# The MLP of a float32 decoder trunk: chunks of W1 interleaved with K tile pairs of W2, both column halves by seven products, sums moved in and out of PSUM

## The chip, the cores and the metric

The kernel runs on one core of one Trainium2 chip, as one program. The metric is the device time of an execution in microseconds. Before the change the runs took 2034.95, 2032.8 and 2032.91 us; their median is 2032.91 us. Each profile is of one further execution.

## What is computed

Two layers over 256 positions of width 2048, in float32. Layer 0 mixes by a gated short convolution, layer 1 by multi-head latent attention. Each mixer and each MLP is followed by a layer norm of `ALPHA * h + f(h)`. The part that the change touches is the MLP of both layers:

```python
def sq_relu_mlp(x, w1, w2):
    return jnp.square(jax.nn.relu(x @ w1)) @ w2    # x: 256 x 2048, w1: 2048 x 8192, w2: 8192 x 2048
```

## The kernel before, in words

**Numbers.** A float32 value is held as a pair: `hi` (rounded to fp32r by ScalarE) and `lo` (the rest, by a VectorE subtraction); `split` (L120) makes one pair and is two instructions. Each product is then three matmuls, hi·hi, hi·lo and lo·hi. Where the moving operand is the activations, its hi and lo lie side by side, so hi·(hi, lo) is one matmul of 512 columns (`high`, L199) and lo·hi is one of 256 columns (`low`, L203). Where the moving operand is the weights, the three are matmuls of 512 columns (`dot`, L271).

**The stream of weights.** All weights come through one list, `stream` (L75), in the order of their use. A *unit* is a tile of 128 x 1024 floats (512 KB), loaded by SyncE into one of five `raw` buffers and split into one of eight pairs of `hi`/`lo` buffers. `take` (L182) hands out the next items and, ahead of them, calls `prepare` (L146) for later items up to five tiles ahead (`LOOK`).

**The MLP before** (`mlp`, L550) goes by eight quarters `q` of 1024 hidden columns. In each, eight *chunks* of 128 hidden columns are made (`products`, L253, called with `lag=False`, so that `high` and `low` alternate for each of the 16 K tiles); a chunk is evacuated by `whole` (L327: a ScalarE copy of one half of the bank, a VectorE add of the other) and then by Relu, Square and a split. In quarter 0 the chunks are made from the not yet normalised input (`mm_wide`). Then the quarter's four *pairs* of K tiles are multiplied by W2. W2's 2048 columns are four blocks of 512 (n = 0 to 3).

- A plain pair-half (two K tiles, two token halves, two column blocks) is 8 `dot`s. `down` (L286) does it block by block, in two PSUM banks.
- A fast pair-half is done by 7 products in place of 8 (a Winograd form of Strassen's scheme on 2 x 2 blocks). `down_fast` (L314) does it, in seven PSUM banks, with the order in `FACTORS` (L311). It needs three more forms of W2 (T1 to T4 with B11, B22 and B21; L161 to L176), and four more of the hidden values (S1 to S4, L604 to L607). For each fast pair-half `prepare` has VectorE do one subtraction of 1024 elements (L165), two of 512 (L168, L171), three `lo` of 1024 and one of 512, and ScalarE the `hi` of the same.
- Before, only columns 0 to 1023 go the fast way, and only in the quarters `FAST` (L36): quarters 1 to 6 of layer 0, 1 to 7 of layer 1. Each has 4 pairs, so that is 24 and 28 fast pair-halves of the 64 in a layer.

At the end of each quarter `combine` (L639) and `put` (L567) add the PSUM sums to `acc` in SBUF, on VectorE. `to_wide` (L655) and `to_out` (L900) take the last quarter of layers 0 and 1; in layer 1 `turn_residual` (L892) puts the transposed residual into `acc` ahead of the last quarter.

**Order.** The tile framework allocates buffers, sets every wait, and orders each engine's queue. Its order can differ from that of the source: in the trace L605 of one pair runs before L331 that the source puts ahead of it.

Of the kernel before, what the change touches and what calls it, by code (L numbers as in the profile page):

```python
# [31 lines left out]
LOOK = 5  # L32
# [3 lines left out]
FAST = {0: range(1, NQ - 1), 1: range(1, NQ)}  # L36
FIRST = ((0, 2, 4, 8), (0, 4, 8))
GROUP = 3
# [4 lines left out]
LAG = 16  # L43
# [4 lines left out]
def trunk(ctx: ExitStack, tc: tile.TileContext, xT, vecs, w_in, w_out, w_kv, w_q, w_uk, w_uv,  # L48
# [12 lines left out]
    ROOM = {"a1": 16896, "a2": 16896, "b": 33280, "c": 16384}  # L61
# [8 lines left out]
    def halves(w):  # L70

        lead = len(w.shape) - 2
        return [(w,)] if lead == 0 else [h for i in range(w.shape[0]) for h in halves(w[i])]
# [5 lines left out]

    def mlp_stream(l):  # L80
        out = []
        for q in range(NQ):
            out += halves(w1[l, q * QC:(q + 1) * QC])
            lead = 0
            if q in FAST[l]:
                out += [(w2f[l, q, j, 0], w2f[l, q, j, 1]) for j in range(QC // 2)]
                lead = 2
            out += halves(w2[l, q, lead:])
        return out
# [4 lines left out]
    stream += halves(w_o) + mlp_stream(1)  # L94

    class Banks:


        more, count = None, 0
# [12 lines left out]
        @classmethod  # L112
        def next(cls):
            cls.count += 1
            return cls.more if cls.more is not None and cls.count % 8 >= 4 else pmm

    state = {"split": 0, "next": 0}
# [13 lines left out]
    def load(i, raw, cuts):  # L131

        hi, lo = ready[i] = parts(i)
        for b0, b1 in zip(cuts, cuts[1:]):
            at, cols = slice(b0, b1), slice(P * b0, P * b1)
            nc.sync.dma_start(raw[:, cols], stream[i][0][:, cols])
            yield
            split(hi[:, at, :], lo[:, at, :], tiled(raw[:, cols]))
            yield
# [6 lines left out]
    def prepare(i):  # L146

        if len(stream[i]) == 1:
            raw = load_raw(i, stream[i][0])
            hi, lo = ready[i] = parts(i)  # L150
            split(hi, lo, tiled(raw))
            return
        r1, r2 = (load_raw(f"{i}_{j}", src) for j, src in enumerate(stream[i]))
        out = []

        def finished(r, name):
            hi, lo = parts(name)
            split(hi, lo, tiled(r))
            out.append((hi, lo))

        b22, (b21, b12) = r1[:, BW:], (r2[:, :BW], r2[:, BW:])  # L161
        finished(r1, f"{i}_1")
# [4 lines left out]
        finished(t, f"{i}_t")  # L167
        nc.vector.tensor_tensor(b12, b22, t[:, :BW], ALU.subtract)  # L168
        finished(r2, f"{i}_2")
        t4 = r1[:, :BW]  # L170
        nc.vector.tensor_tensor(t4, b21, b12, ALU.subtract)  # L171
        f = state["fast"].tile([P, 2, BW], F32R, tag="t4", name=f"t4_{i}")
        split(f[:, 0, :], f[:, 1, :], t4)
        b1, t13, b2 = ([[v.rearrange("p b c -> p (b c)")[:, o:o + BW] for v in w] for o in (0, BW)] for w in out)
        ready[i] = {"11": b1[0], "22": b1[1], "21": b2[0], "T2": b2[1], "T1": t13[0], "T3": t13[1],
                    "T4": [f[:, 0, :], f[:, 1, :]]}  # L176

    def size(i):

        return 1 if len(stream[i]) == 1 else 3  # L180

    def take(halves=2):  # L182

        i = state["next"]
        state["next"] += halves
        ahead = -sum(size(j) for j in range(i, i + halves))
        for j in range(i, len(stream)):
            ahead += size(j)
            if ahead > LOOK:
                break  # L190
            if j >= state["split"]:
                prepare(j)
                state["split"] = j + 1
        return [ready.pop(i + j) for j in range(halves)]
# [12 lines left out]
    def mm_run(wps, x, k0, k1, nk, tiles_first=False, turn=None):  # L207
# [4 lines left out]
        for k, (w, ps) in order:  # L212
            if k == turn:
                low(ps, w, k, x[k], False)
                high(ps, w, k, x[k], False)
                continue
            high(ps, w, k, x[k], k == 0)
            low(ps, w, k, x[k], k == nk - 1)

    def mm_lag(ps, w, x):  # L220

        for k in range(NC + LAG):
            if k < NC:
                high(ps, w, k, x[k], k == 0)
            if k >= LAG:
                low(ps, w, k - LAG, x[k - LAG], k == NC + LAG - 1)

# [25 lines left out]
    def products(n, x, group=0, cuts=(), turn=None, lag=True):  # L253
# [7 lines left out]
        for i in range(group, n):  # L261
            w = take()
            ps = psum("ps_u")
            if lag:
                mm_lag(ps, w, x)
            else:
                mm_run([(w, ps)], x, 0, NC, NC, turn=turn if i == 0 else None)
# [3 lines left out]
    def dot(ps, w, x, first, last):  # L271

        nc.tensor.matmul(ps, x[0], w[0], start=first, stop=False)  # L273
        nc.tensor.matmul(ps, x[0], w[1], start=False, stop=False)  # L274
        nc.tensor.matmul(ps, x[1], w[0], start=False, stop=last)  # L275
# [34 lines left out]

    FACTORS = (("4", "22", "T4"), ("2", "12", "21"), ("3", "S4", "22"), ("1", "11", "11"),  # L311
               ("6", "S2", "T2"), ("7", "S3", "T3"), ("5", "S1", "T1"))

    def down_fast(x, forms):  # L314

        ps = {p: psum(f"ps_f{p}") for p, _, _ in FACTORS}
        n = len(x) // 2
        for j in range(n):
            b, = take(1)
            a = {"11": held(x[2 * j], 0), "12": held(x[2 * j + 1], 0), "22": held(x[2 * j + 1], 1)}  # L320
            for i in range(4):
                a[f"S{i + 1}"] = [v[:, j, (4 + i) * P:(5 + i) * P] for v in forms]
            for p, l, r in FACTORS:
                dot(ps[p], b[r], a[l], j == 0, j == n - 1)
        return ps
# [191 lines left out]
    state["split"] = 2 * GROUP  # L517
# [32 lines left out]
    def mlp(idx, ln, begin, blocks, fast):  # L550
# [12 lines left out]

        def block(n, t):
            return acc[:, t, n * BW:(n + 1) * BW]

        def put(n, t, ps):  # L567
            if q == 0:
                nc.scalar.copy(block(n, t), ps)
                for _ in range(2):  # L570
                    normal()
            else:
                nc.vector.tensor_tensor(block(n, t), block(n, t), ps, ALU.add)

        for q in range(NQ):
            forms = [array(a, F32R, f"h{idx}_{q}_{a}", QC // 2, 8 * P) for a in ("c", "a2")] if q else None
            if q == NQ - 1:
                begin(block)
            if forms is None:
                ht = array("c", F32R, f"h{idx}_{q}", QC, 2 * T)  # L580
                h = [ht[:, k, :] for k in range(QC)]
            else:
                h = [tuple(v[:, k // 2, (k % 2) * T:(k % 2 + 1) * T] for v in forms) for k in range(QC)]

            def hidden(m, ps, evac, *func):
                if forms is None:
                    f = tmp.tile([P, T], F32, tag="fh", name="fh", bufs=3)
                else:
                    if m % 2 == 0:
                        state["pair"] = fast.tile([P, 8 * P], F32, tag="sf", name="sf")  # L590
                    f = state["pair"][:, m % 2 * T:(m % 2 + 1) * T]
                evac(ps, f, *func)
                if not func:
                    nc.scalar.activation(f, f, AF.Relu)  # L594
                nc.scalar.activation(f, f, AF.Square)
                if forms is None:
                    put_split(h[m], f)
                elif m % 2:
                    hi, lo = (v[:, m // 2, :] for v in forms)
                    src, cols = state["pair"], 4 * P  # L600
                    if q in FAST[idx // 2]:
                        cols = 8 * P
                        a11, a21, a12, a22, s1, s2, s3, s4 = (src[:, i * P:(i + 1) * P] for i in range(8))
                        nc.vector.tensor_tensor(s1, a21, a22, ALU.add)  # L604
                        nc.vector.tensor_tensor(s3, a21, a11, ALU.subtract)  # L605
                        nc.vector.tensor_tensor(s2, s1, a11, ALU.subtract)
                        nc.vector.tensor_tensor(s4, a12, s2, ALU.subtract)  # L607
                    split(hi[:, :cols], lo[:, :cols], src[:, :cols])

            if q == 0:  # L610
                for m in range(QC):
                    if m < GROUP:
                        if m == 0:
                            ws = ln.ws if ln.ws else group_of(GROUP)
                            if not ln.ws:
                                mm_wide(ws, ln.xd)
                            ln.finish()
# [6 lines left out]
                    if m > 0:  # L624
                        normal()
# [393 lines left out]
```

## Time and profile before

| | us |
|---|---|
| median of three runs | 2032.91 |
| the profiled execution | 2034.58 |
| its span, first to last instruction | 2032.5 |
| PE busy, 11208 matmuls | 2013.5 |
| VectorE (DVE) busy | 1654.6 |
| ScalarE (ACT) busy | 1181.9 |
| moved by DMA | 385.31 MB |

The profile lists engines as PE (matmul), PEld (weight load, beside PE), DVE, ACT, POOL and SP. A group's row gives line, engine, operation, output<-inputs, shape and count; then the busy time in us, the mean ns of one, and the idle time just before. Consecutive instructions of one engine overlap by some tens of ns, so costs per instruction are read from start to start. A matmul's listed length is longer still than its pace, since matmuls are pipelined.

### The profile page before, as it was taken

To read this page: it belongs to the slowest core of one execution; us is meant where nothing else is said; L and a number is where in the kernel's file an instruction comes from. 1 tells how busy PE (TensorE), PEld (TensorE's weight loads), DVE (VectorE), ACT (ScalarE), POOL (GpSimd) and SP (SyncE) were. 2 spreads that over 40 slices of the span, in tenths; PEclk is the share of its full clock that TensorE was granted. 3 is DMA by queue.
4 is the path that set the end of the run, shared out by engine and by line. 5 is a ranking of instruction groups with operands and counts; after the bars stand their busy time and mean duration, and the time that the engine had idled before them with its cause. 6 is when DMAs were issued, how large, how long until landed. Compare 5 with 4: busy or idle time off the path is not lost.

```text
span 2032.5 us, 30055 instructions
## 1 busy us (share of the span) xinstructions
PE 2013.5 (99%) x11208; PEld 1760.0 (87%) x11208; DVE 1654.6 (81%) x2494; ACT 1181.9 (58%) x1752; POOL 2.3 (0%) x21
## 2 busy tenths in 40 slices
PE   9999999999999999999999999999999999999997
PEld 7888888988888888888889998898888888888885
DVE  7667667677898988989688888777889898898988
ACT  6444445576565565655556655467656566565652
POOL 0000000000000000000000000000000000000000
PEclk9999999999999999999999999999999999999998
DMA  8666656564746557475754534656475665746644
GB/s 297 204 190 189 191 189 190 166 202 139 254 145 227 181 182 254 145 233 174 230 176 149 176 122 134 199 171 201 137 248 152 221 210 161 250 145 224 206 164 152
DMA packets 108002, 385.31 MB, mean 190 GB/s; under 512 B 11984, under 2 KB 13392, under 8 KB 107856
## 3 DMA queue, kind: packets, MB, share of 16 engines
q1 hardware_dynamic: 107712, 383.13, 58.8%
q8 instruction: 88, 1.44, 0.3%
q14 instruction: 58, 0.48, 0.1%
q10 hardware_dynamic: 144, 0.26, 0.0%
HBM read 381.25 MB, written 2.10 MB: 189 GB/s over the span
## 4 chain that ended last, share of the span: by engine, by line
PE 96%; DVE 2%; DMA 1%; issue 1%; ACT 0%; DVEq 0%; ACTq 0%
PE ps_u L201 32%; PE ps_u L205 17%; PE ps_d L273 7%; PE ps_d L274 7%; PE ps_d L275 7%; PE ps_f L274 4%; PE ps_f L275 4%; PE ps_f L273 4%; PE ps_w L247 1%; PE ps_w L245 1%; PE ps_w L246 1%; PE ps_g L247 1%; PE ps_g L245 1%; PE ps_g L246 1%; DMA raw<-in_w2f_dram 1%
## 5 line engine op out<-in xcount | busy, mean ns | idle before, releaser
L123 DVE TENSOR_TENSOR lo<-raw,hi 128x1024 fp32r<-128x1024 f32 x712 | 856.9, 1221 | 257.7 <-ACT hi L122 179.9
L122 ACT CAST hi<-raw 128x1024 fp32r<-128x1024 f32 x712 | 743.6, 1051 | 486.4 <-PE ps_u L201 268.9
L201 PE MATMUL ps_u<-xhl,hi 128*128 128x512 f32 x1792 | 622.1, 392 | 0.0
L205 PE MATMUL ps_u<-xhl,lo 128*128 128x256 f32 x1792 | 499.6, 280 | 0.0
L201 PEld LDWEIGHTS ps_u<-xhl,hi 128*128 128x128 f32 x1792 | 334.4, 187 | 73.1
L205 PEld LDWEIGHTS ps_u<-xhl,lo 128*128 128x128 f32 x1792 | 338.6, 189 | 1.7
L273 PE MATMUL ps_d<-hi,h_c 128*128 128x512 f32 x480 | 186.8, 389 | 0.0
L275 PE MATMUL ps_d<-hi,h_a 128*128 128x512 f32 x480 | 186.6, 389 | 0.0
L274 PE MATMUL ps_d<-lo,h_c 128*128 128x512 f32 x480 | 186.6, 389 | 0.0
L201 PE MATMUL ps_u<-xhl_a,hi 128*128 128x512 f32 x720 | 171.9, 391 | 0.0
L201 PEld LDWEIGHTS ps_u<-xhl_a,hi 128*128 128x128 f32 x720 | 132.4, 188 | 25.7
L274 PEld LDWEIGHTS ps_d<-lo,h_c 128*128 128x128 f32 x480 | 90.1, 188 | 18.8 <-DVE lo L123 0.2
L275 PEld LDWEIGHTS ps_d<-hi,h_a 128*128 128x128 f32 x480 | 90.1, 188 | 18.7
L273 PEld LDWEIGHTS ps_d<-hi,h_c 128*128 128x128 f32 x480 | 90.1, 188 | 18.6
L205 PEld LDWEIGHTS ps_u<-xhl_a,lo 128*128 128x128 f32 x720 | 92.3, 191 | 3.5
L594 ACT ACTIVATE sf<-sf 128x256 f32<-128x256 f32 x112 | 46.7, 417 | 82.1 <-DVE sf L331 81.9
L205 PE MATMUL ps_u<-xhl_a,lo 128*128 128x256 f32 x720 | 93.4, 283 | 0.0
L122 ACT CAST hi_t<-raw_t 128x1024 fp32r<-128x1024 f32 x52 | 54.6, 1050 | 47.1 <-DVE raw_t L165 32.0
L330 ACT COPY t<-ps_u 128x256 f32<-128x256 f32 x157 | 57.0, 363 | 42.1 <-PE ps_u L205 42.1
L274 PE MATMUL ps_f<-lo,h_c 128*128 128x512 f32 x208 | 81.2, 390 | 0.2 <-DVE lo L123 0.2
L275 PE MATMUL ps_f<-hi,h_a 128*128 128x512 f32 x208 | 81.1, 390 | 0.0
L273 PE MATMUL ps_f<-hi,h_c 128*128 128x512 f32 x208 | 80.7, 389 | 0.0
(235 smaller groups left out, 3290.8 us busy)
## 6 DMA issues: line engine op xcount, KB each, us to landing
raw<-in_w_dram SPq DMA_DIRECT2D x408, 512.0 KB, 4.4
raw<-in_w2f_dram SPq DMA_DIRECT2D x104, 512.0 KB, 3.6
raw<-in_w_in_dram SPq DMA_DIRECT2D x90, 512.0 KB, 4.2
raw<-in_w_out_dram SPq DMA_DIRECT2D x32, 512.0 KB, 4.0
raw<-in_w_o_dram SPq DMA_DIRECT2D x32, 512.0 KB, 4.1
raw<-in_w_kv_dram SPq DMA_DIRECT2D x10, 512.0 KB, 4.2
raw<-in_w_q_dram SPq DMA_DIRECT2D x8, 512.0 KB, 4.4
raw<-in_w_uk_dram SPq DMA_DIRECT2D x8, 512.0 KB, 4.5
```

The lines of the kernel that those rows point to most:

```text
L122: nc.scalar.copy(hi, src)
L123: nc.vector.tensor_tensor(lo, src, hi.bitcast(F32), ALU.subtract)
L201: nc.tensor.matmul(ps, w[blk // 8][0][:, blk % 8, :], x, start=first, stop=False)
L205: nc.tensor.matmul(ps[:, :T], w[blk // 8][1][:, blk % 8, :], x[:, :T], start=False, stop=last)
L245: nc.tensor.matmul(ps[:, :W], hi, x[k][:, :W], start=k == 0, stop=False)
L246: nc.tensor.matmul(ps[:, :W], lo, x[k][:, :W], start=False, stop=False)
L247: nc.tensor.matmul(ps[:, :W], hi, x[k][:, W:], start=False, stop=k == NC - 1)
L273: nc.tensor.matmul(ps, x[0], w[0], start=first, stop=False)
L274: nc.tensor.matmul(ps, x[0], w[1], start=False, stop=False)
L275: nc.tensor.matmul(ps, x[1], w[0], start=False, stop=last)
L330: nc.scalar.copy(t, ps[:, T:])
L594: nc.scalar.activation(f, f, AF.Relu)
```

## The change

The quarters go. After the first eight chunks a plan alternates one *group* (one pair-half of W2) with one chunk of W1, to the end of the 28 first pairs (`KEPT`); the three chunks that remain follow, and the last four pairs are done by `down` in all four column blocks.

- **Fast almost everywhere.** Both column halves (b = 0: columns 0 to 1023; b = 1: the others) go the fast way, save the pairs in `PLAIN`: 0 and 1 in both halves, and 4, 8, 12, 16, 20, 24 in half 1. A layer has 46 fast and 10 plain groups.
- **Turns.** The halves take turns of four pairs (the first turn is of two). The seven sums of one half stay in seven PSUM banks; at a turn ScalarE copies each to a slot of 512 columns in SBUF (`spill`) and copies the other half's back into the bank (`seed`), and the next matmuls go on adding to it. A plain group inside half 1 uses bank 1 for C22, so one spill and one seed stand after it too.
- **Folding once a layer.** `fold` and `combine` add the seven sums up at the end, in 16 VectorE adds; before, each quarter did so.
- **One bank for W1.** While the seven banks are held, all chunks of W1 share the eighth (`Banks.only`).
- **Chunks** are now 8 `high`, 8 `low`, 8 `high`, 8 `low` (`mm_like`). In the mixers 16 `high` and then 16 `low` follow each other, as before.
- **The stream** is prepared tile by tile (`prepare` is a generator) up to eight tiles from the start of the item in use. `sf` and `t4` have two buffers, each other buffer count is kept.
- **Moved:** the norm's preparation of layer 0 is spread over the groups, the other half of the normalised input is made in the first four groups, and `turn_residual` now comes after the fold.

```diff
+PAIRS = FF // (2 * P)
+KEPT = PAIRS - QC // 2
+SLOTS = 10
+PLAIN = ((0, 1), (0, 1, *range(4, KEPT, 4)))
...
+    def plan():
+        nxt, b, steps, m, count = [0, 0], 0, [], QC, 0
+        while min(nxt) < KEPT:
+            end = min(nxt[b] + (4 if nxt != [0, 0] else 2), KEPT)
+            run = [(b, j, j in PLAIN[b]) for j in range(nxt[b], end)]
+            for i, (b, j, plain) in enumerate(run):
+                steps.append(("group", b, j, plain, i == 0, i == len(run) - 1))
+                if count >= 3 and m < FF // P:
+                    steps.append(("m", m))
+                    m += 1
+                count += 1
+            nxt[b], b = end, 1 - b
+        return steps + [("m", i) for i in range(m, FF // P)]
...
+        while state["made"] < min(start[i] + WA, start[-1]):
+            next(making)
+            state["made"] += 1
...
+    def mm_like(ps, w, x, n=NC):
+        for h in range(0, NC, n):
+            for k in range(h, h + n):
                 high(ps, w, k, x[k], k == 0)
+            for k in range(h, h + n):
+                low(ps, w, k, x[k], k == NC - 1)
...
+    FAST = (("1", "11", "11"), ("3", "S4", "22"), ("7", "S3", "T3"), ("5", "S1", "T1"),
+            ("2", "12", "21"), ("6", "S2", "T2"), ("4", "22", "T4"))
...
+        def spill(self, p):
+            if p in self.live:
+                nc.scalar.copy(self.slot(self.live.pop(p)), self.bank[p])
+
+        def seed(self, p, key):
+            if key in self.store:
+                nc.scalar.copy(self.bank[p], self.at(key))
+                self.drop(key)
+                self.live[p] = key
...
+        def turn(self, b, plain):
+            for p, _, _ in FAST:
+                if p in self.bank:
+                    self.spill(p)
+                    self.seed(p, (b, "C" if p == "1" and plain else p))
...
+            if step[0] == "m":
+                w, ps = take(), psum("ps_m")
+                mm_like(ps, w, xhl, 8)
...
+                whole(ps, half)
+                if m % 2:
+                    nc.scalar.activation(f[:, :4 * P], f[:, :4 * P], AF.Relu)
+                    square(f)
...
+            w, = take(1)
+            later = [s for s in steps[at + 1:] if s[0] == "group"]
+            turns = plain and bool(later) and not later[0][3]
+            sums.group(b, w, parts_of(j), plain, last, turns)
+            if later:
+                if last:
+                    sums.turn(later[0][1], later[0][3])
+                elif turns:
+                    sums.spill("1")
+                    sums.seed("1", (b, "1"))
```

More of the change, by code (lines that the diff above doesn't have):

```diff
@@ L31 @@
 NEG = -1e30
-LOOK = 5
 RAW, WA = 5, 8
@@ L94, in trunk @@
     stream += halves(w_o) + mlp_stream(1)
+    size = {"unit": 1, "plain": 2, "fast": 3}
+    start = [0]
+    for kind, *_ in stream:
+        start.append(start[-1] + size[kind])
     class Banks:
-        more, count = None, 0
+        more, count, only = None, 0, None
         @classmethod
@@ new lines, in mlp @@
+        sums = Sums(idx)
+        Banks.only = Banks.more
+        count = 0
+        for at, step in enumerate(steps):
+            if step[0] == "m":
+                m = step[1]
+                w, ps = take(), psum("ps_m")
+                mm_like(ps, w, xhl, 8)
+                if m % 2 == 0:
+                    f = pair()
+                half = f[:, m % 2 * T:(m % 2 + 1) * T]
+                whole(ps, half)
+                if m % 2:
+                    nc.scalar.activation(f[:, :4 * P], f[:, :4 * P], AF.Relu)
+                    square(f)
+                    j, cols = m // 2, 4 * P
+                    if j < KEPT:
+                        forms(f)
+                        cols = 8 * P
+                    split(one[:, j % 4, :cols], two[:, j % 4, :cols], f[:, :cols])
+                if m == FF // P - 3:
+                    Banks.only = None
+                continue
+            _, b, j, plain, first, last = step
+            w, = take(1)
[8 more added lines that the diff above has]
+                    sums.seed("1", (b, "1"))
+            if first and j + 4 >= KEPT and b == 0 and j + 2 >= KEPT:
+                folded = sums.fold(1)
+            if not later:
+                folded = sums.combine(0) + folded
+            if count < 4:
+                normal()
+                normal()
+            if hook is not None:
+                hook(count)
+            count += 1
@@ L564, in block @@
         def block(n, t):
-            return acc[:, t, n * BW:(n + 1) * BW]
+            return folded[n][t]
         def put(n, t, ps):
[L568 to L617, printed above, removed]
-                        ps = ws[m][1]
-                    else:
-                        ws = [(take(), psum("ps_w"))]
-                        mm_wide(ws, ln.xd)
-                        ps = ws[0][1]
-                    hidden(m, ps, ln.weighted, AF.Relu)
-                    if m > 0:
-                        normal()
-                acc = array("a1", F32, f"acc{idx}", 2, D)
-            else:
-                for m, ps in enumerate(products(QC, xhl, turn=2, lag=False)):
-                    hidden(m, ps, whole)
-            if q == NQ - 1:
-                blocks(block, put, h, forms)
-                return
-            if q in FAST[idx // 2]:
-                combine(put, down_fast(h, forms))
-            for n in range(2 if q in FAST[idx // 2] else 0, NB):
-                down(h, put, n)
@@ L657, in turned, with to_wide @@
+        h = [(one[:, k // 2, k % 2 * T:(k % 2 + 1) * T], two[:, k // 2, k % 2 * T:(k % 2 + 1) * T]) for k in range(QC)]
+        blocks(block, put, h)
+    def to_wide(block, put, h):
         def turned(n):
```

273 lines of the change are left out of this document (169 added, 104 removed).

## The prediction

> **What bounds the kernel now.** I read the page's totals and slices first, then who waits for whom, then the pace of PE in each kind of stage, then what the other engines have left there.
>
> ```profile
> span 2032.5 us, 30055 instructions
> ...
> PE 2013.5 (99%) x11208; PEld 1760.0 (87%) x11208; DVE 1654.6 (81%) x2494; ACT 1181.9 (58%) x1752; POOL 2.3 (0%) x21
> ...
> DVE  7667667677898988989688888777889898898988
> ```
>
> PE has no hole, and the DVE digits show 8 and 9 just in the two MLPs: a second engine is close behind. PE's waits are few:
>
> ```profile
> PE ps_g L201 <- DVE xhl_a L336: 2.5, 2, 1.7
> PE warm L349 <- DVE col L351: 1.1, 1, 1.1
> PE ps_g L201 <- ACT hi L122: 0.8, 1, 0.8
> PE lnAB L372 <- DVE rr L367: 0.3, 1, 0.3
> ```
> ```profile
> PE 96%; DVE 2%; DMA 1%; issue 1%; ACT 0%; DVEq 0%; ACTq 0%
> ```
>
> (Waits: total us, times, longest; those left out are shorter. Below them the chain that ended last, by engine.) Time goes down one for one with matmuls removed, as long as the others feed PE.
>
> A "busy" PE counts modelled lengths, so its pace is read from starts. Two timelines of PE, `dot`s and an MLP chunk (first and last row of 57 and of 27 starts), and the chain in the mixer:
>
> ```profile
> 519.68 0.39 PE L274 MATMUL ps_f<-lo,h_c 128*128 128x512 f32 x1
> ...
> 532.37 0.39 PE L273 MATMUL ps_d<-hi,h_c 128*128 128x512 f32 x1
> ```
> ```profile
> 477.79 0.39 PE L201 MATMUL ps_u<-xhl,hi 128*128 128x512 f32 x1
> ...
> 486.80 0.39 PE L201 MATMUL ps_u<-xhl,hi 128*128 128x512 f32 x1
> ```
> ```profile
> 99.77 3.65 PE ps_u L201 x16
> 103.42 1.91 PE ps_u L205 x16
> ```
>
> A `dot` matmul: 12.69 us / 56 = 0.2266 us. An alternating `high`/`low` pair: 9.01 / 26 = 0.3465, so 5.545 us a chunk. Sixteen of each in a row: 3.65 + 1.91 = 5.56 us. So a fast group is 21 x 0.2266 = 4.76 us, a plain one 24 x 0.2266 = 5.44 us.
>
> How near DVE is shows in stretches of one fast quarter each (length, PE, PEld, DVE, ACT busy):
>
> ```profile
> 544.40:629.80 85.40, 85.40 (x439) 73.03 (x438) 74.41 (x96) 51.81 (x70) 0.00 (x0) 1.00 0.61 199
> 629.80:715.20 85.40, 85.40 (x439) 73.08 (x438) 73.86 (x96) 50.89 (x70) 0.00 (x0) 1.00 0.60 195
> ```
>
> DVE 87%, ACT 60%, PE without a wait, clock 1.00.
>
> **The change, part by part.** *Removed matmuls.* Fast pair-halves go from 24 + 28 = 52 to 46 + 46 = 92. Forty `dot`s fewer, 120 matmuls, 11088 in all: 120 x 0.2266 = **-27.2 us**.
>
> *Chunk order.* 112 chunks from 5.545 to 5.56: **+1.7** (0 to 3; with 8 and 8 it lies between the two rows).
>
> *DVE.* Costs from start to start come from the groups (busy, mean ns) and from unbroken runs, one of DVE and one of ACT:
>
> ```profile
> L123 DVE TENSOR_TENSOR lo<-raw,hi 128x1024 fp32r<-128x1024 f32 x712 | 856.9, 1221 | 257.7 <-ACT hi L122 179.9 <-issue 38.4 <-PE ps_u L205 37.5
> ...
> L165 DVE TENSOR_TENSOR raw_t<-raw,raw 128x1024 f32<-128x1024 f32 x52 | 63.4, 1220 | 4.5 <-DMA raw<-in_w2f_dram 4.2
> L573 DVE TENSOR_TENSOR acc<-acc,ps_f 128x512 f32<-128x512 f32 x78 | 52.1, 681 | 0.4
> L331 DVE TENSOR_TENSOR sf<-ps_u,t 128x256 f32<-128x256 f32 x112 | 46.8, 418 | 0.3 <-ACT t L330 0.3
> L573 DVE TENSOR_TENSOR acc<-acc,ps_d 128x512 f32<-128x512 f32 x60 | 40.4, 684 | 3.8 <-PE ps_d L275 3.7
> L171 DVE TENSOR_TENSOR raw<-raw 128x512 f32<-128x512 f32 x52 | 35.6, 686 | 0.5
> ...
> L573 DVE TENSOR_TENSOR acc<-acc,vu 128x512 f32<-128x512 f32 x39 | 25.6, 684 | 0.0
> ...
> L606 DVE TENSOR_TENSOR sf<-sf 128x128 f32<-128x128 f32 x52 | 15.0, 288 | 0.9
> ```
> ```profile
> 517.21 3.49 DVE L123 TENSOR_TENSOR lo<-raw,hi 128x1024 fp32r<-128x1024 f32 x3
> ```
> ```profile
> 513.71 1.05 ACT L122 CAST hi<-raw 128x1024 fp32r<-128x1024 f32 x1
> 514.66 0.62 ACT L122 CAST t<-raw 128x512 fp32r<-128x512 f32 x1
> 515.18 1.99 ACT L122 CAST hi<-raw 128x1024 fp32r<-128x1024 f32 x2
> ```
>
> Three `lo` take 3.49, where three lengths are 3.66, so each overlaps the next by 0.085: DVE pays 1.135 us for 1024 elements, 0.60 for 512, 0.335 for 256, 0.20 for 128. ACT pays 0.95 for 1024, 0.52 for 512.
>
> - Fast group, DVE: three `lo` and one subtraction of 1024, one `lo` and two subtractions of 512: 4 x 1.135 + 3 x 0.60 = 6.34 us. Plain group: 2.27.
> - Chunk: two `lo` and the add of `whole`, 2.6; for every second chunk the S forms (0.2 + 0.335 + 0.2) and a split of 1024, so 0.93 a chunk.
> - A step of group and chunk: fast 9.88 us of DVE beside 4.76 + 5.56 = 10.32 of PE; plain 5.81 beside 11.0.
>
> A cycle of eight steps, a turn of each half, has seven fast and one plain: **DVE 75.0, PE 83.2 us, 90%**. So DVE alone doesn't become the bound, though it has less left than now. It is given back the adds of each quarter (78 + 60 + 39 of L573 at about 0.60, against 24 per layer); the fold's 16 lie beside the last groups and chunks.
>
> *ACT and the turns.* A turn is 7 spills and 7 seeds. By the plan a layer has 12 full turns, two part ones and the pairs of copies after plain groups: 195 copies, 390 in all. The nearest row for a spill is the second one here, a copy out of PSUM of that shape; the first is the copy of `whole`:
>
> ```profile
> L330 ACT COPY t<-ps_u 128x256 f32<-128x256 f32 x157 | 57.0, 363 | 42.1 <-PE ps_u L205 42.1
> ...
> L569 ACT COPY acc<-ps_d 128x512 f32<-128x512 f32 x16 | 9.0, 582 | 4.2 <-PE ps_d L275 3.9
> ```
>
> 582 ns less the same overlap is 0.49. A copy into PSUM is in no row; between that row and the cast (0.52) I take 0.52, so a turn is 7 x 1.01 = 7.1 us. By the Trainium skill, "ScalarE: Activation LUTs", section "What ACT_TABLE_LOAD costs", an ACTIVATE with immediate operands takes 186 ns + 0.833 ns per element and overlaps the next by 93 ns; that would make 0.52 us of each copy (an estimate) and 7.3 us of a turn, and this trace's 582 ns lies just under it.
>
> ACT per cycle: fast step 3 x 0.95 + 0.52, chunk 1.9 + 0.3 (363 ns less the overlap), half of (Relu, Square, split of 1024) 1.0, so 6.6; plain 5.1; with two turns and one extra pair 7 x 6.6 + 5.1 + 15.2 = 66.5 of 83.2, 80%.
>
> The copies wait for PE: a spill of a bank waits for that bank's last `dot`, 0.68 us after the one before, while a spill and a seed take 1.01, so ACT is held 7.1 us and ends some 8 us after the group began. PE comes back to bank 1 after 10.3 us: the seeds themselves hide behind the chunk. What is queued behind them on ACT are the casts of the next tiles; DVE's `lo` waits for these:
>
> ```profile
> DVE lo L123 <- ACT hi L122: 183.6, 179, 5.6
> ...
> ACT hi L122 <- DMA raw<-in_w_dram: 126.0, 137, 2.8
> ```
>
> Call s the time that DVE idles in a turn: at most 7.1. Meanwhile it can do the next fast pair's first two subtractions (1.74), a chunk's add (0.33) and one or two `lo` whose cast is ready (1.1 to 2.3): 3.2 to 4.3 us, so s is 2.8 to 3.9. The cycle then needs 75.0 + 2s = 80.6 to 82.8 us of DVE, just inside PE's 83.2. Eight buffers of tiles cover the turn itself. Timing isn't that even (loads land late, an odd chunk costs 1.9 more than an even one), so I take 0.3 us of PE wait for each of 24 full turns: **+7** (0 to 72, below).
>
> *Starts and ends.* The first three groups of a layer have no chunk between, so bank 3's spill (0.5) stands open, and eight normalisations wait beside four plain groups; after the last chunk the folded block must be ready, in layer 1 after 8 more DVE operations of 0.6 us (the moved residual, whose 32 transposes PE does as before). 0 to 4 us a layer, I take 2: **+4**.
>
> *Loads.*
>
> ```profile
> raw<-in_w2f_dram SPq DMA_DIRECT2D x104, 512.0 KB, 3.6
> ```
>
> The same bytes in the same tiles of 512 KB from SP's queue, 3.6 us to land, 4 per step: 2.1 MB in 10.3 us, 203 GB/s, beside 199 in the stretch above. Hidden, if `raw` buffers come free in time; there are still five.
>
> Sum: -27.2 + 1.7 + 7 + 4 = **-14.5**. The profiled execution took 2034.58 us (2.1 beyond its span), so 2020.1; it lies 1.7 above the median of the runs, 2032.91, so the forecast is **2018 us**.
>
> **The rivals.**
>
> *ACT's turns starve DVE (slower).* Place: the casts behind 14 copies. Price: 12 cycles x (75.0 + 2s - 83.2). With the other terms at -21.5 it decides at 1.8 us a cycle, s = 5.0. At s = 6 it costs 46 us: 2034.6 - 21.5 + 46 = 2059, **2057** against the median; at 7.1, 72 us. For it: DVE's longest idle before a cast is 5.6 us already, and a cast needs a `raw` that DVE has freed, so ACT can't run far ahead. Against: the queue's order isn't the source's, so casts can stand between the copies, and PE never waited at 87% DVE. By the Trainium skill, "PSUM — Partial Sum Buffer", section "Engine vs sequencer instructions", ScalarE's queue is strictly first in, first out: a spill that waits holds all behind it. By that rule s goes to the upper end wherever copies stand in one block.
>
> *The one bank for W1.* The next chunk needs ACT's copy and DVE's add within the 4.76 us of a group. Before, PE ends a quarter's chunks at 503.26; counted back by 5.545 us each, chunks end at 481.08 and 497.72, and their adds:
>
> ```profile
> 503.26 0.23 PE ps_f L273
> ```
> ```profile
> 481.61 0.42 DVE L331 TENSOR_TENSOR sf<-ps_u,t 128x256 f32<-128x256 f32 x1
> ...
> 503.70 0.42 DVE L331 TENSOR_TENSOR sf<-ps_u,t 128x256 f32<-128x256 f32 x1
> ```
>
> They are done 1.0 and 6.4 us after their chunk. The second would now cost 6.4 - 4.76 = 1.6 us. One in eight of 106 chunks is 21 us: 2034.6 - 21.5 + 21 = 2034, **2032** against the median, no change. Against: nothing waited for that bank then.
>
> *PE never waits.* 2034.6 - 27.2 + 1.7 = 2009, **2008** against the median. For it: PE's record now. Against: DVE at 90% plus turns.
>
> *The matmuls aren't saved.* A count other than 11088 would show it; the plan's counts leave it under 1 in 100.
>
> **How the numbers follow.** Two tenths of a per cent, about 4 us, is what a measurement of this kernel can tell from no change: 2028.8 to 2037.0. Forecast (2010 to 2027) 0.47; PE never waits 0.16; one bank, about 2032, 0.10; starved DVE, over 2037, 0.27. Faster 0.63, same 0.10, slower 0.27. The range, 2004 to 2052, leaves out the half of the slow case with s over 5.8, and little below.
>
> **What would show it.** Right: 11088 matmuls; cycles of 83 to 84 us; ACT near 80% and DVE near 90% there; PE's waits in the MLPs about 10 us in sum, next to turns. The starved case: PE waiting for `lo` or `hi` after turns, cycles over 85 us, and DVE idle 5 us or more per turn behind casts. The one-bank case: PE's waits at `ps_m` for the add of `whole`, in any step. The forecast is wrong too if a copy into PSUM takes much over 0.6 us, since ACT then fills the step, or if the loads of fast pairs land too late for five `raw` buffers.

## The result and the profile after

The changed kernel takes 2040.6 us (median of six runs, 2038.4 to 2041.95), the kernel before on the same chips 2032.72 (2032.5 to 2034.95): ratio 1.0036 [1.0025, 1.0048]. It is 7.9 us slower, where 14.5 us faster was forecast. The profiled execution took 2041.95 us, with a span of 2040.0.

The page's totals, the slices of VectorE and, from the chain of work that ended last, the shares by engine:

```profile
span 2040.0 us, 30047 instructions
...
PE 2003.0 (98%) x11088; PEld 1740.1 (85%) x11088; DVE 1717.1 (84%) x2483; ACT 1386.8 (68%) x2071; POOL 2.3 (0%) x21
...
DVE  7667677799889898898878888779898988989886
```
```profile
PE 61%; DVE 18%; DMA 10%; ACT 6%; issue 4%; DVEq 0%; SPq 0%; ACTq 0%
```

The 120 matmuls are gone, yet the span grew. Before, 96% of the chain lay on PE; now a fifth of it lies on DVE, a tenth on transfers, some on ACT. So PE gets its operands late. Two successive cycles of eight steps each (length; busy time of PE, PEld, DVE, ACT and POOL; clock; DMA share; GB/s):

```profile
567.30:653.70 86.40, 84.86 (x429) 71.17 (x429) 78.50 (x93) 68.97 (x98) 0.00 (x0) 1.00 0.62 199
653.70:740.20 86.50, 84.23 (x429) 71.12 (x428) 77.78 (x93) 68.69 (x97) 0.00 (x0) 1.00 0.60 197
```

PE's own work in a cycle is 83.2 us by the pace of its matmuls (83.5 as measured in `no_copies_raw6` below, where PE hardly waits in the MLPs). Over the twelve cycles of the two MLPs the mean length, taken from the first matmul of each eighth chunk to the next, is 86.3: 3.1 us too long, 37 us in all, against the 27.2 that the removed matmuls give. PE's waits (us in total, times, longest), first those of its matmuls, then among the rows of all engines:

```profile
PE sum L296 <- ACT sum L589: 18.0, 18, 2.5
PE ps_m L231 <- DVE sf L338: 2.8, 2, 2.3
```
```profile
DVE lo L145 <- ACT hi L144: 95.8, 99, 5.6
ACT hi_t L144 <- DVE raw_t L195: 85.0, 46, 3.2
ACT hi L144 <- DMA raw<-in_w2f_dram: 59.9, 57, 2.7
...
DVE raw_t L195 <- DMA raw<-in_w2f_dram: 46.2, 52, 2.5
...
PEld sum L296 <- ACT sum L589: 29.8, 32, 3.0
```

Read from the last wait backwards. PE waits at `sum` for a seed (L589), a copy of ACT. ACT in turn waits 85.0 us for DVE's first subtraction of a fast pair (`raw_t`, L195) and 59.9 us for loads of `w2f`; that subtraction waits for loads, 46.2 us in 52 cases, where it was 4.2 us in all before. Such a wait is no loss by itself: before, ACT waited 126.0 us for loads (the row stands in the prediction) and PE didn't wait. What is new is that DVE waits too, and that the seeds stand in ACT's queue behind the casts. What fell is DVE's wait for casts: 95.8, from 183.6. The copies themselves are as expected (count, busy, mean ns), and so is their number, 390:

```profile
L585 ACT COPY sums<-sum 128x512 f32<-128x512 f32 x204 | 118.5, 587 | 3.5 <-PE sum L298 2.6
L589 ACT COPY sum<-sums 128x512 f32<-128x512 f32 x186 | 111.5, 599 | 1.4
```

One turn in the timeline of ACT; the turn's first copy starts at 887.25, its last ends at 905.98:

```profile
887.25 0.59 ACT L585 COPY sums<-sum 128x512 f32<-128x512 f32 x1
887.72 1.05 ACT L144 CAST hi<-raw 128x1024 fp32r<-128x1024 f32 x1
...
895.51 0.60 ACT L589 COPY sum<-sums 128x512 f32<-128x512 f32 x1
897.07 1.05 ACT L144 CAST hi<-raw 128x1024 fp32r<-128x1024 f32 x1 [0.96 <-PE sum L298]
...
898.76 0.60 ACT L589 COPY sum<-sums 128x512 f32<-128x512 f32 x1
...
905.39 0.59 ACT L589 COPY sum<-sums 128x512 f32<-128x512 f32 x1
```

In the same stretch DVE's subtraction waits for its load, and PE for the fourth seed (898.76 to 899.36):

```profile
892.90 1.23 DVE L195 TENSOR_TENSOR raw_t<-raw,raw 128x1024 f32<-128x1024 f32 x1 [1.44 <-DMA raw<-in_w2f_dram]
```
```profile
899.42 0.50 PE L296 MATMUL sum<-hi_t,hc 128*128 128x512 f32 x1 [1.71 <-ACT sum L589]
```

The copies don't stand in a block: ten casts of the next tiles lie between them, so a turn takes 18.7 us and not 7.1. In this turn ACT hardly idles (0.96 us, for PE), so it isn't a wait inside the turn that makes the fourth seed late: ACT comes to the turn late. `raw7` below shows the same turn without that delay.

### The profile page after: what moved, and what is told of

It reads as the page before. It is cut to its first block, busy times and chain, and to the rows that moved or that the text cites. A ratio compares the mean times of both kernels' runs of the same rounds, so it can differ in the third digit from the quotient of the medians.

```text
span 2040.0 us, 30047 instructions
## 1 busy us (share of the span) xinstructions
PE 2003.0 (98%) x11088; PEld 1740.1 (85%) x11088; DVE 1717.1 (84%) x2483; ACT 1386.8 (68%) x2071; POOL 2.3 (0%) x21
## 4 chain that ended last, share of the span: by engine, by line
PE 61%; DVE 18%; DMA 10%; ACT 6%; issue 4%; DVEq 0%; SPq 0%; ACTq 0%
PE ps_u L231 13%; PE ps_m L231 9%; DMA raw<-in_w2f_dram 9%; PE ps_u L235 7%; DVE lo L145 6%; PE ps_m L235 4%; PE sum L296 3%; PE sum L298 3%; PE sum L297 3%; ACT hi L144 3%; DVE raw_t L195 2%; DVE lo_t L145 2%; DVE ha L145 2%; PE ps_d L296 1%; PE ps_d L298 1%
## 5 line engine op out<-in xcount | busy, mean ns | idle before, releaser
L231 PE MATMUL ps_m<-xhl,hi 128*128 128x512 f32 x1792 | 455.1, 393 | 2.9 <-DVE sf L338 2.8
L231 PEld LDWEIGHTS ps_m<-xhl,hi 128*128 128x128 f32 x1792 | 330.1, 189 | 70.6 <-DVE sf L338 6.2
L235 PEld LDWEIGHTS ps_m<-xhl,lo 128*128 128x128 f32 x1792 | 245.2, 190 | 18.1
L235 PE MATMUL ps_m<-xhl,lo 128*128 128x256 f32 x1792 | 250.9, 282 | 0.0
L296 PE MATMUL sum<-hi,hc 128*128 128x512 f32 x512 | 202.6, 396 | 7.3 <-ACT sum L589 7.3
L297 PE MATMUL sum<-lo,hc 128*128 128x512 f32 x512 | 200.7, 392 | 0.0
L298 PE MATMUL sum<-hi,ha 128*128 128x512 f32 x448 | 173.3, 390 | 0.0
L195 DVE TENSOR_TENSOR raw_t<-raw,raw 128x1024 f32<-128x1024 f32 x92 | 112.5, 1223 | 46.9 <-DMA raw<-in_w2f_dram 46.2
L585 ACT COPY sums<-sum 128x512 f32<-128x512 f32 x204 | 118.5, 587 | 3.5 <-PE sum L298 2.6
L589 ACT COPY sum<-sums 128x512 f32<-128x512 f32 x186 | 111.5, 599 | 1.4
L145 DVE TENSOR_TENSOR lo_t<-raw_t,hi_t 128x1024 fp32r<-128x1024 f32 x92 | 112.1, 1219 | 0.0
L296 PE MATMUL sum<-hi_t,hc 128*128 128x512 f32 x168 | 66.5, 396 | 10.5 <-ACT sum L589 10.4
```

The costliest lines, as they stand in the source:

```text
L145: nc.vector.tensor_tensor(lo, src, hi.bitcast(F32), ALU.subtract)
L195: nc.vector.tensor_tensor(t.rearrange(two, a=2), b12.unsqueeze(1).to_broadcast([P, 2, BW]), r1.rearrange(two, a=2), ALU.subtract)
L231: nc.tensor.matmul(ps, w[blk // 8][0][:, blk % 8, :], x, start=first, stop=False)
L235: nc.tensor.matmul(ps[:, :T], w[blk // 8][1][:, blk % 8, :], x[:, :T], start=False, stop=last)
L296: nc.tensor.matmul(ps, x[0], w[0], start=first, stop=False, skip_group_check=goes_on)
L297: nc.tensor.matmul(ps, x[0], w[1], start=False, stop=False, skip_group_check=goes_on)
```

## The experiments

The theory after this reading: **loads come too late**, because a fast pair holds three of five `raw` buffers (two for its loads, L164, and one for `t`, L193) while the chunks go on beside it; the copies make it worse, since they are queued behind casts that wait for loads. Rivals: the copies alone (ACT's time), copies that starve DVE, DVE that is too full, and one bank for W1. Ratios are to the kernel before.

### Without the copies, and with copies that feed nobody

Either all spills and seeds are left out, or each seed copies a slot onto itself, so that ACT has the same work and PE doesn't wait for it.

```
no_copies:    spill: self.slot(self.live.pop(p))       seed: no copy
              nc.gpsimd.memset(self.room, 0.0), once a layer
dummy_seeds:  seed: nc.scalar.copy(self.at(key), self.at(key))
```

> Leaves out all spills and seeds (the sums of the two halves run into each other in the banks; the slots in SBUF are only zeroed once), all else as in the changed kernel. Theory 1, PE waits for seeds that come late: those waits (about 25 us in both MLPs) go, and with ScalarE at the old load nearly all of the 27 us of removed matmuls shows: 2010 to 2016 us. Rival, VectorE and the loads of fast pairs set the pace and the seed is only where PE happens to wait: 2030 us or more.

> Each seed is a copy of its SBUF slot onto itself: ScalarE has the same number of copies of the same size at the same places, but no bank is written back (the sums of the halves run into each other), so PE waits for spills at most. Theory 1a, it is the way spill, then seed, then PE that is late: 2012 to 2022 us. Theory 1b, it is ScalarE's load as such, which holds the casts: 2033 to 2042 us, with PE's waits moved to hi and lo tiles or to the chunk's bank.

`no_copies`: 2019.71 us, 0.9929 [0.9915, 0.9944]. `dummy_seeds`: 2054.32, 1.0100 [1.0085, 1.0116], slower than the change. Both lie outside what was expected: 2019.7 between the two ranges, 2054 above both. The copies cost 20.9 us, but without them the kernel still isn't at the 2008 of "PE never waits". The waits of `no_copies`, and PE's of `dummy_seeds`:

```profile
PE ps_m L231 <- DVE sf L338: 6.6, 13, 1.4
```
```profile
DVE raw_t L195 <- DMA raw<-in_w2f_dram: 60.8, 46, 3.0
```
```profile
PE ps_m L231 <- DVE sf L338: 25.9, 19, 2.5
```

DVE still waits for loads with no copy in the queue. With dummy seeds PE's wait moves to the one bank of W1, where DVE's add is late: that wait is where a late DVE shows. The one bank isn't a cause by itself: `no_copies_raw6` below keeps it, and PE's matmuls don't wait for it there. Why `dummy_seeds` is slower than the change wasn't shown.

### The copies in a block

Here the next bank's spill stands ahead of this bank's seed, and the turn is given precedence in ACT's order (`turn_block`). `turn_paired` has the same without the precedence. Both need an eleventh slot, paid for by a buffer of `fh` and by `COL`; `fh2` has only these two sizes.

```
-SLOTS = 10            +SLOTS = 11
-COL = 128             +COL = 8
-tag="fh", bufs=3      +tag="fh", bufs=2
 turn: spill(first); spill(next), seed(this), ...; seed(last)
 turn_block: with tc.high_priority(offset=400)
```

> Same work, other order: at a turn the spill of the next bank is issued ahead of the seed of this one, with raised priority, so that the 14 copies of a turn stand next to each other in ScalarE's queue instead of alternating with casts (this takes an eleventh slot; two small buffers give the room). Theory 1a: a turn takes some 7 to 8 us instead of 18, seeds are in before PE comes back, PE's waits for seeds fall under 3 us in all: 2012 to 2022 us. The prediction's starved VectorE: casts are held 7 us in each turn, VectorE idles 4 us or more, PE waits for lo tiles instead: 2035 us or more.

> As the block, but without raised priority: casts still slip in between some copies, the turn is shorter than in the changed kernel and longer than in the block. Theory 1a: between the block and the changed kernel, 2016 to 2032 us. Starved VectorE: as the changed kernel or better than the block.

> The changed kernel with what turn_block and turn_paired gave up for their eleventh slot (two fh buffers in place of three, eleven slots of which ten are used), and the turn's order as it was. If it is the order that made those two slow: 2037 to 2046 us. If it is the smaller buffer: 2060 us or more.

`turn_block`: 2114.23 us, 1.0395 [1.038, 1.0411]. `turn_paired`: 2063.63, 1.0144 [1.0127, 1.0161]. `fh2`: 2062.37, 1.0146 [1.0131, 1.0161]. So the sizes alone account for `turn_paired`, and the block costs 2114.23 - 2062.37 = 52 us over `fh2`. ACT's timeline in `turn_block`, then its waits:

```profile
587.21 0.59 ACT L585 COPY sums<-sum 128x512 f32<-128x512 f32 x1 [0.47 <-PE sum L298]
...
588.44 1.11 ACT L589 COPY sum<-sums 128x512 f32<-128x512 f32 x2
...
592.44 1.14 ACT L589 COPY sum<-sums 128x512 f32<-128x512 f32 x2
```
```profile
DVE sf L338 <- ACT t L337: 66.8, 13, 5.9
...
DVE lo_t L145 <- ACT hi_t L144: 49.0, 10, 5.6
```

Fourteen copies in 6.4 us, and then DVE idle 5 us on average behind a cast (49.0 in 10) or the copy of a chunk (66.8 in 13), about once in each of 24 full turns: this is the rival "ACT's turns starve DVE". Its price in the prediction at s = 5 is 12 x 1.8 = 22 us. Up to another 21 of the 52 go with the clock: the mean granted clock of the profiled executions is 0.985 over 2110.5 us in `turn_block` and 0.995 over 2060.9 in `fh2`, so 31.7 and 10.3 us of full clock are missing (an estimate). It is a true mechanism, but not that of the change, whose copies let casts through. The Trainium skill, "PSUM — Partial Sum Buffer", section "Engine vs sequencer instructions", has ScalarE's queue strictly first in, first out; the 66.8 us behind an unbroken block agree.

### Less of DVE's work

If DVE were too full, it would help to make a second group in each turn of half 1 plain (4.07 us less DVE a cycle, 6.34 - 2.27, for three more matmuls; 36 more in all), or to move one subtraction to GpSimd.

```
plain2:  PLAIN[1] = (0, 1, *[j for j in range(4, KEPT) if j % 4 < 2])
pool_t4: L199  nc.gpsimd.tensor_tensor(b11, b21, b12, ALU.subtract)
```

> Two plain groups in each turn of half 1 in place of one: 12 fast groups fewer, 36 matmuls more (8.2 us of PE), VectorE 4.1 and ScalarE 1.5 us less for each. If VectorE and ScalarE limit the cycle of eight groups (86.3 us measured, 83.2 of PE): PE needs 83.9, VectorE 70.9, and the cycle falls to 84 to 85.5, the kernel to 2020 to 2034 us. If PE's waits have to do with the copies alone, which stay as they are: 2045 to 2050 us.

> One of the two subtractions of 512 elements of each fast group (the one for T4) on GpSimd, which is idle, in place of VectorE: 0.6 us less for VectorE in each fast step, 4.2 in a cycle. If VectorE's load limits the cycle and the two engines don't slow each other: 2022 to 2036 us. If GpSimd is slow or slows VectorE: 2040 us or more, with longer VectorE instructions in the trace.

`plain2`: 2063.03 us, 1.0148 [1.0119, 1.0177], above both ranges; its `raw_t` waits 85.1 us for loads, more than in the change. `pool_t4`: 2134.64, 1.0496 [1.048, 1.0511]. The subtraction and two of DVE's groups in `pool_t4` (busy, mean ns):

```profile
L199 POOL TENSOR_TENSOR raw<-raw 128x512 f32<-128x512 f32 x92 | 182.6, 1985 | 1570.3 <-DVE raw L197 782.5 <-DVE lo L145 735.5 <-DMA raw<-in_w_dram 33.8
```
```profile
L145 DVE TENSOR_TENSOR lo_t<-raw_t,hi_t 128x1024 fp32r<-128x1024 f32 x92 | 139.5, 1516 | 8.3 <-ACT hi_t L144 8.3
...
L145 DVE TENSOR_TENSOR ha<-sf,hc 128x1024 fp32r<-128x1024 f32 x48 | 81.5, 1698 | 0.0
```

GpSimd needs 1985 ns where DVE takes 688 (below), and DVE's own instructions beside it become longer: 1516 and 1698, where in the change, with the subtraction on DVE:

```profile
L145 DVE TENSOR_TENSOR lo_t<-raw_t,hi_t 128x1024 fp32r<-128x1024 f32 x92 | 112.1, 1219 | 0.0
L199 DVE TENSOR_TENSOR raw<-raw 128x512 f32<-128x512 f32 x92 | 63.3, 688 | 1.4
...
L145 DVE TENSOR_TENSOR ha<-sf,hc 128x1024 fp32r<-128x1024 f32 x48 | 58.5, 1219 | 1.4 <-ACT hc L144 1.4
```

Neither edit relieves what is late. `pool_t4` didn't test the theory of a full DVE well, since it made both engines slower.

### Earlier loads

A sixth `raw` buffer, paid for by one `t4` buffer; a seventh, paid for by one `sf` buffer too. The kernel before gets the sixth as well, and `no_copies` does.

```
raw6:  RAW, WA = 6, 8; t4 bufs=1          raw7:  RAW, WA = 7, 8; t4 bufs=1; sf bufs=1
no_copies_raw6, plain2_raw6, plain2_raw7: both edits
before_raw6: the kernel before, RAW, WA = 6, 8
```

> A sixth raw buffer for loads, paid for by one t4 buffer in place of two, all else as in the changed kernel. If late loads of fast pairs set VectorE's pace (it stood idle 46 us before the first subtraction of a pair, waiting for a load): that idle time falls under 15 us and the kernel to 2025 to 2036 us. If ScalarE's order and load alone do: 2036 to 2045 us, and the idle time only moves elsewhere.

> Both of the former. If loads and VectorE's load each hold up PE: below both, 2014 to 2030 us. If it is the copies alone: 2045 us or more.

> No spills and no seeds (as in no_copies, so the sums of the halves run into each other) and a sixth raw buffer (as in raw6). If copies and late loads are all that stands between the changed kernel and the count of its matmuls: 2008 to 2013 us, PE's waits in the MLPs under 3 us. If VectorE's load of 90% costs by itself: 2015 us or more.

> The kernel before with a sixth raw buffer and nothing else. PE never waited there, so nothing is to be had: 2031 to 2035 us. If it gets faster by more than 4 us, then the sixth buffer's gain isn't the change's own.

> Seven raw buffers, paid for by one t4 and one sf buffer, all else as in the changed kernel. If late loads still cost something with six (VectorE still stood idle 20 us before first subtractions): 2016 to 2024 us. If what is left is the copies' share of ScalarE: 2023 to 2028 us.

> Two plain groups in each turn of half 1 and seven raw buffers (one t4, one sf). With six it was 2024.8 us, 84.9 us a cycle where PE needs 83.9. If the loads are the rest of it: 2018 to 2023 us. If not: 2023 to 2028 us.

| kernel | us | ratio to before |
|---|---|---|
| change, five buffers | 2040.6 | 1.0036 [1.0025, 1.0048] |
| `raw6` | 2025.27 | 0.9960 [0.9945, 0.9975] |
| `raw7` | 2011.65 | 0.9903 [0.9887, 0.9920] |
| `plain2_raw6` | 2024.77 | 0.9959 [0.9944, 0.9974] |
| `plain2_raw7` | 2020.99 | 0.9943 [0.9928, 0.9957] |
| `no_copies_raw6` | 2007.18 | 0.9873 [0.9859, 0.9888] |
| `before_raw6` | 2045.68 | 1.0064 [1.0049, 1.0079] |

With seven buffers the change is 21.2 us faster than the kernel before (2032.87 there). Without copies five buffers give 2019.7 and six 2007.2, so late loads cost 12.5 where no copies stand in the queue (the six also have one `t4` buffer less); with five buffers the copies cost 20.9, with six 18.1 (2025.27 - 2007.18), with seven 4.5 against the same kernel. Of `raw7` the shares of the chain, one cycle and waits:

```profile
PE 91%; DVE 5%; ACT 2%; DMA 2%; issue 1%; DVEq 0%; ACTq 0%
```
```profile
812.50:896.20 83.70, 83.70 (x429) 71.12 (x428) 77.07 (x94) 69.29 (x98) 0.00 (x0) 1.00 0.62 204
```
```profile
DVE raw_t L195 <- DMA raw<-in_w2f_dram: 8.9, 12, 1.4
...
PEld sum L296 <- ACT sum L589: 7.3, 27, 0.9
```

The load wait falls from 46.2 to 8.9, that for the seeds from 29.8 to 7.3, the cycle to 83.7. How long a load takes isn't it: the `w2f` loads land 4.0 us after their issue in the change (median) and 4.8 in `raw7`. SP's own waits, first of the change, then of `raw7`, show one place where the loads stood:

```profile
SPq L165 <- DVE lo_t L145: 338.9, 78, 6.9
```
```profile
SPq L165 <- DVE lo_t L145: 90.3, 24, 5.7
```

By the releaser that the profile names, the next load waits for the buffer that held `t`, which DVE frees with `lo_t`, 78 times in the change and 24 in `raw7`. This row doesn't rank the kernels by itself: `raw6` still has 80 such waits, 311.2 us.

Early loads change where a turn starts. The turn above, in ACT's timeline of `raw7` (first copy, fourth seed, last copy):

```profile
871.53 0.59 ACT L585 COPY sums<-sum 128x512 f32<-128x512 f32 x1 [0.32 <-PE sum L298]
...
881.46 0.60 ACT L589 COPY sum<-sums 128x512 f32<-128x512 f32 x1
...
889.46 0.62 ACT L589 COPY sum<-sums 128x512 f32<-128x512 f32 x1
```

It takes 18.6 us, as long as in the change, with eleven casts in it. But here ACT has been waiting for PE, and the first copy starts 0.9 us after the group's first matmul (870.63); in the change it starts 2.1 us after it (885.13) and ACT didn't wait. The fourth seed is done 1.1 us into PE's next group (880.98) in `raw7` and 3.9 us into it (895.48) in the change, where PE asks for it some 2 us into it. Over the 24 full turns the first copy starts 0.86 us (median) after the matmuls that it waits for have ended in the change, 1.97 in `small5` below, and 0.04 in `raw6` and `raw7`.

A load that lands late inside a turn does the same harm. One of `raw6`, whose first copy is on time (833.68): the next three lines are of DVE, ACT and PE.

```profile
836.86 1.23 DVE L195 TENSOR_TENSOR raw_t<-raw,raw 128x1024 f32<-128x1024 f32 x1 [2.19 <-DMA raw<-in_w2f_dram]
```
```profile
839.88 1.05 ACT L144 CAST hc<-sf 128x1024 fp32r<-128x1024 f32 x1 [1.96 <-DVE sf L669]
```
```profile
847.60 0.51 PE L296 MATMUL sum<-hi,hc 128*128 128x512 f32 x1 [1.79 <-ACT sum L589]
```

DVE waits for the load; the last of the S forms (L669) stands behind that subtraction on DVE; ACT's cast waits for it, and the seeds stand behind the cast. The order of the queues shifts with the buffers too (in the turn above ten casts and eleven), so order and lead aren't wholly separated.

Some expectations failed. `raw7` is faster than its range, and the first subtraction of `raw6` still waits 19.9 us for loads, where under 15 was expected. `before_raw6` is above its range: a sixth buffer makes the kernel before 12.8 us slower, with PE waiting 6.1 us for adds of `acc`. A buffer more is no gain in every kernel; why it costs there wasn't settled.

### Buffers alone, and without the plain groups

What stayed open: `raw7` also took away a `t4` and an `sf` buffer. So these two sizes with five and six `raw` buffers, and, to test a full DVE, `raw7` with no plain group beyond the first two.

```
small5, small6:  t4 bufs=1; sf bufs=1; RAW, WA = 5, 8 or 6, 8
raw7_fast:       raw7 with PLAIN = ((0, 1), (0, 1))
```

> The changed kernel with one sf and one t4 buffer in place of two each, and raw left at five: what raw7 gave up, without what it got for it. If the raw buffers are the cause, this is no better than the changed kernel: 2038 to 2060 us. If the single sf and t4 buffers gave the gain by another order of the queues: 2010 to 2025 us.

> The same with six raw buffers. If the raw buffers are the cause, it lies between small5 and raw7: 2015 to 2035 us. Otherwise near small5.

> Seven raw buffers, and half 1 without its plain groups after the first two: 6 fast groups more in each layer, 36 matmuls fewer (8.2 us of PE). A cycle is then 82.6 us of PE, and about 79 of VectorE by the prediction's costs (96%). If VectorE holds its pace: 2002 to 2008 us, the fastest of all. If 96% is too much: 2012 us or more, with PE's waits back.

`small5`: 2051.68 us, 1.0104 [1.0077, 1.0130]. `small6`: 2024.02, 0.9957 [0.9943, 0.9972]. `raw7_fast`: 2001.85, 0.9848 [0.9834, 0.9863]. With all else equal, five, six and seven buffers give 2051.7, 2024.0 and 2011.7. The waits for loads of `small5` and `small6`:

```profile
ACT hi L144 <- DMA raw<-in_w2f_dram: 82.1, 66, 2.5
DVE raw_t L195 <- DMA raw<-in_w2f_dram: 26.8, 28, 1.8
```
```profile
DVE raw_t L195 <- DMA raw<-in_w2f_dram: 17.6, 26, 2.2
...
ACT hi L144 <- DMA raw<-in_w2f_dram: 3.4, 2, 1.8
```

108.9 us of waiting for `w2f`, then 21.0, then 8.9 in `raw7` (DVE's; ACT has no such row there). In this series the time follows the waits. It doesn't across kernels: `no_copies` waits 99.7 us for `w2f` and takes 2019.7, `no_copies_raw6` 49.4 and takes 2007.2. So what a wait for a load costs PE isn't read from its length. And `raw7_fast`, 80 us of it:

```profile
720.00:800.00 80.00, 80.00 (x408) 67.98 (x407) 77.00 (x94) 65.95 (x92) 0.00 (x0) 1.00 0.63 203
```

DVE is busy 96%, more than in any cycle above (at most 91% in the change, 92% in `raw7`), and PE doesn't wait. A full DVE is no cause. This version beats both kernels: 30.9 us less than the kernel before.

## Why the prediction was wrong

- **Removed matmuls, -27.2: right.** 11088, and where PE hardly waits in the MLPs (`no_copies_raw6`) the kernel is at 2007.2, against the 2008 of "PE never waits" (2007.4 by its own sum).
- **Chunk order, +1.7: right, but smaller, 1.1.** From start to start, a chunk that nothing interrupts takes 5.549 us in a fast quarter before and 5.559 in the change (medians), 0.010 more for each of 112.
- **Starts and ends, +4: about 0.4.** 2032.9 - 27.2 + 1.1 is 2006.8, and `no_copies_raw6`, which has the same starts and ends without their copies, takes 2007.2 (an estimate).
- **DVE, nothing by itself: right.** 75.0 us a cycle were worked out; 77 to 78 are busy, and 96% in `raw7_fast` holds PE up no more.
- **Size of the copies: right.** 390 copies of 587 and 599 ns, as against 582 from the row of before; ACT 68.9 us busy in a cycle for 66.5.
- **Turns, +7: right where loads are early, failed in the change.** From `no_copies_raw6` to `raw7` it is 4.5 us, 0.19 a full turn where 0.3 was taken; only roughly, since the two differ in a `raw` and an `sf` buffer as well. In the change it is 20.9, and 18.1 in `raw6`. "The seeds themselves hide behind the chunk" took 14 copies as a block that starts as soon as PE frees the first bank. They alternate with casts, so a turn takes 18.7 us; that alone is nearly hidden in `raw7`. In the change ACT also starts the turn late, and in `raw6` a cast inside a turn still waits behind a late load.
- **Loads, nothing: this is the step that failed.** "Hidden, if `raw` buffers come free in time; there are still five." They don't come free in time. The bytes per second were compared (203 beside 199), but not how many buffers a step holds, and for how long. By a count from the kernels (how long each buffer is held wasn't measured): before, a fast quarter filled 36 buffers in 85.4 us (four pairs of three, 8 plain units, 16 of W1); now a cycle fills 39 in 83.2 us (seven pairs of three, a plain one of two, 16), at the same 32 loads, since each fast pair's `t` takes a buffer that no load fills. Two buffers are worth 2051.7 - 2011.7 = 40 us at otherwise equal sizes, and `raw7` is 2040.6 - 2011.65 = 29 us below the change, which is more than the 22.6 by which the forecast missed. The sum closes: in place of 7 and 0 the turns and the loads cost 20.9 and 12.5, and chunk order and starts and ends 4.2 less than taken, 22.2 us more in all, from 2018.4 to 2040.6. Where the loads are early (`raw7`), the forecast of 2018 is 6.4 us off, in turns, chunk order and starts and ends, all taken too high. The condition stood among the things that would make the forecast wrong, without a price or a chance.
- **The rivals.** Starved DVE: the change is slower, as it said, and cycles are over 85 us, but its mechanism isn't that of the change (DVE's wait for casts fell); it shows in `turn_block`. One bank: PE's waits at `ps_m` are 2.8 us in the change and 25.9 in `dummy_seeds`, and none in `no_copies_raw6`, which has the one bank too. PE never waits: true in `no_copies_raw6`.

What stays open: at five buffers edits that change no work on the path move the time by 11 to 22 us (`small5` +11, `dummy_seeds` +14, `fh2` +22; `plain2` +22, of which 36 more matmuls make 8.2). Late loads and a fixed order in each queue are common to them; which instruction costs how much in each wasn't shown. A part is the clock (below): its mean is 0.994 in `dummy_seeds` and 0.995 in `fh2` where it is 0.997 in the change, up to 6 and 4 us (estimates from these shares of the span). Nor was it shown what slows `before_raw6`.

## What to carry to other kernels

A transfer that is as fast as before isn't hidden for that: count the buffers that a step holds between its load and the last reader, and when the next load can be issued, as you count busy time. When copies are added to an engine's queue, read where they stand among the work already there; the same turns of 14 copies cost 21, 18 and some 5 us a kernel with five, six and seven buffers, and 52 more when they stood in one block, in part by the clock. If "hidden, if ..." stands in a sum, the condition needs a price and a chance.

## What the runs showed of the hardware

After a wait of PE of 2.31 us the granted clock falls to half for 3.4 us. Windows of the change (columns as above), then PE's timeline at the end of that wait and at full clock:

```profile
507.47:510.88 3.41, 1.10 (x6) 0.60 (x5) 3.41 (x5) 3.41 (x7) 0.00 (x0) 1.00 0.19 52
510.89:514.29 3.40, 3.40 (x10) 2.69 (x9) 2.39 (x3) 2.48 (x6) 0.00 (x0) 0.50 0.78 233
514.30:518.00 3.70, 3.70 (x21) 3.17 (x20) 1.44 (x2) 3.54 (x6) 0.00 (x0) 1.00 0.58 185
```
```profile
510.46 3.45 PE L231 MATMUL ps_m<-xhl,hi 128*128 128x512 f32 x8 [2.31 <-DVE sf L338]
...
889.92 1.98 PE L231 MATMUL ps_m<-xhl,hi 128*128 128x512 f32 x8
```

The same eight matmuls take 3.45 us there and 1.98 at full clock, so this wait costs some 1.5 us more than its length. The length alone doesn't decide: in `raw6` a wait of 1.79 us (to 847.60) is followed by 3.4 us at 0.50, and in the change one of 1.92 us (to 812.85) by full clock. The Trainium skill, "TensorE: Matmul & The Clock Gate", section "What's actually happening", has the gate at 4/8 after an idle window of about 3.4 us; the 0.50 and the 3.4 us agree, but the waits that set it off were shorter than that window. In `pool_t4` the mean granted clock is 0.983 over 2129.2 us, so up to 30 of its 94 us over the change go with the clock (an estimate, as for `turn_block`).

A ScalarE copy of 128x512 from SBUF into PSUM takes 599 ns, one from PSUM into SBUF 587, and one within SBUF 629 (`dummy_seeds`). The 512-element subtraction of GpSimd takes 2.9 times that of DVE (1985 and 688 ns) and makes DVE's two-operand instructions beside it longer by 24 to 39%. The Trainium skill, "GPSIMD Engine Reference", section "1. Specifications", says that GpSimd shares its SBUF interfaces with VectorE, with contention for instructions with two SBUF inputs; these rows agree.
